# Two table streams in one kernel: a shorter lag, fetches over 8 tokens, routing of all but one head inside the stream

## The chip, the cores and the metric

The kernel runs on one core of one Trainium2 chip. The metric is the time of one execution on the device, in microseconds. The core's engines are named as in the profile: PE is TensorE, DVE is VectorE, ACT is ScalarE, POOL is GpSimd, SP is SyncE. PE, DVE, ACT and POOL each execute their own list of instructions in order and wait on semaphores for one another. Data come from HBM through 16 DMA engines; a transfer is issued from the queue of one of the engines, here from SP (weights) and from POOL (table rows).

## The reference

Two transformer blocks for 256 tokens of 2048 values, all in float32. The first has two kinds of attention and, behind them, a mixture of single-row experts; the second has two more mixers. The change lies in the mixture of experts alone. For each token and each of 8 heads it searches 16 experts among 16384, takes the dot of the token with their rows in one table (`expert_u`), and adds up their rows of a second table (`expert_v`) with weights from these dots:

```python
def peer_ffn(h, w_q, sub_keys, expert_u, expert_v):
    q = (hf @ w_q).reshape(t, PEER_HEADS, 2, PEER_HALF).astype(jnp.float32)
    s1 = jnp.einsum('thd,nd->thn', q[:, :, 0], sk[0])
    s2 = jnp.einsum('thd,nd->thn', q[:, :, 1], sk[1])
    v1, i1 = lax.top_k(s1, PEER_TOPK)
    v2, i2 = lax.top_k(s2, PEER_TOPK)
    cand = (v1[..., :, None] + v2[..., None, :]).reshape(t, PEER_HEADS, PEER_TOPK * PEER_TOPK)
    cs, ci = lax.top_k(cand, PEER_TOPK)
    row = jnp.take_along_axis(i1, ci // PEER_TOPK, axis=-1)
    col = jnp.take_along_axis(i2, ci % PEER_TOPK, axis=-1)
    experts = row * PEER_NKEYS + col
    gates = jax.nn.softmax(cs, axis=-1)
    ...
        a = jax.nn.gelu(jnp.einsum('chkd,cd->chk', expert_u[ec], hc).astype(jnp.float32))
        w = (gc * a).astype(hc.dtype)
        return jnp.einsum('chk,chkd->cd', w, expert_v[ec])
```

With 256 tokens, 8 heads and 16 experts these are 32768 rows of 8 KB from each table, 537 MB in all.

## The kernel before, in words

**Projections.** Each projection is a `dense` (L170): the weights come in parts of 512 KB, which SP fetches (L106) into one of four `raw` buffers up to three parts ahead. ACT writes the high half of a part (L109), DVE subtracts it to get the low half (L110, "the subtraction"), both into one of four `hl` buffers, and PE multiplies the two halves with the two halves of the activations in three matmuls (L166 to L168) for each of the two token groups of 128, t = 0 and t = 1. A weight with blocks of 512 columns has two steps of 128 rows in a part, so a block of 2048 rows has eight parts. When a block is complete, its two groups are handed to an evacuation, a generator that the loop advances at every part.

**The mixture of experts, `peer` (L634).** Its query projection `w_qp` has four blocks of 512 columns, two heads each. The evacuation `ev_qp` (L730) copies the block out of PSUM, transposes it on PE, and multiplies with the two sets of keys into scores. For t = 0 the routing (`route`, L682) follows right there, for two heads at once: the top 16 of four rows of 128 scores, of two rows of 256 sums, then the ids, by comparisons and products on DVE. The scores of t = 1 are parked in the fourth quarter of the tile `gslot`. The ids stand in `eidx`, one column for each expert of a token group: a fetch of the first table takes one column, so it brings one expert row for each of 128 tokens ("u"). For the second table 32 ids of each token are transposed into `eidv` (`spread`, L675: a transpose on PE, four copies), so that one fetch brings all 32 experts of four tokens ("v").

**The stream.** `fill` (L773) issues the fetches from POOL (L786) in the order of the list `seq`: u alone at first, and from u36 on one v after each u, 36 behind (`VLAG`). It stops when no buffer is free or the ids of the next u have not been computed. A fetch takes a whole buffer of 1 MB: three quarters of `gslot` and one part of `hj` (`gbc`) while the projection runs, the four `hl` buffers (`hg`) in addition when it has ended, and the quarter with the parked scores when these have been used. During the projection a `hook` after every second part uses one u. `use_u` (L809) is one DVE row, the dot of 128 tokens with their expert rows (L812). After 32 dots of a group, `weights` (L797) makes their weights: gelu on ACT, the product with the gates, `spread`, and one DVE product with a mask into `lw`, the left operands of eight v. `use_v` (L818) takes two v at a time and lets PE add them into four PSUM tiles, eight matmuls for each (L828). A buffer is free again when its dot or its eight matmuls are done. The routing of t = 1 is advanced between the uses, from use 40 on, one block of two heads at a time. In the last 16 uses the `hl` buffers go back to the weights of the next block.

**What sets the order.** PE's and POOL's instructions in the stream stand in the order in which the program is written; those of DVE and ACT are ordered by a scheduler's priorities.

## Time and profile of the kernel before

| | us |
|---|---|
| median of 3 runs (lowest to highest) | 2880.39 (2880.06 to 2881.32) |
| the profiled execution, its own time | 2880.4 |
| its span in the trace | 2878.6 |

| engine | busy us | share of the span |
|---|---|---|
| PE | 2307.9 | 80% |
| DVE | 1679.5 | 58% |
| ACT | 791.2 | 27% |
| POOL | 668.8 | 23% |

The profile is of one execution. All its times count from the start of the span, which is 1.8 us shorter than the execution's time. The shares are means over stages with different limits, so they say little: the table stage, from about 715 to 2060 us, has to be read in stretches. The views used here are the timeline of an engine (start of a row, its duration, the instruction, and in brackets the idle time before it with what ended it), a table of stretches, the waits, and the traffic of the DMA queues. Rows on DVE overlap a little, so distances between starts are better prices than durations.

### The profile page before, as it was taken

Reading aid. Unit: us, or ns where it says so; the run is one execution under the profiler, and the core shown is the slowest. Engines: PE = TensorE matmul, PEld = TensorE weight load, DVE = VectorE, ACT = ScalarE, POOL = GpSimd, SP = SyncE. Lnnn points to the kernel's source line nnn. Section 1 sums busy time; section 2 is a strip of 40 time slices with the busy share of each in tenths; the row PEclk is TensorE's granted clock in tenths of the full one; section 3 lists DMA queues with packets and bytes.
Section 4 is the critical chain, followed back from the end, with each engine's and each line's share of the span. In section 5 each row is a group of like instructions: output and inputs, shape, how many; then the busy total and the mean of one; then the engine's idle time right before and its main releaser. Section 6 shows DMA issues by size and latency. Waiting matters only on the chain.

```text
span 2878.6 us, 26351 instructions
## 1 busy us (share of the span) xinstructions
PE 2307.9 (80%) x9488; PEld 1445.4 (50%) x9488; DVE 1679.5 (58%) x2503; ACT 791.2 (27%) x1245; POOL 668.8 (23%) x570
## 2 busy tenths in 40 slices
PE   9999999999515565556666666657899999999999
PEld 7878788888401111111111111111388888888887
DVE  5665755657999644444445444441365566667754
ACT  6544544444200000000000000000244444447743
POOL 0000000000354554445445353534100000001000
PEclk9999999999857878887787878788999999999999
DMA  7545466555989999999999999999755555553355
GB/s 249 171 146 183 151 225 199 185 187 194 353 325 357 407 422 421 422 421 421 422 421 422 422 421 422 422 421 421 290 193 188 170 172 188 187 174 131 121 183 168
DMA packets 151955, 820.24 MB, mean 285 GB/s; under 512 B 17232, under 2 KB 17264, under 8 KB 85776
## 3 DMA queue, kind: packets, MB, share of 16 engines
q0 software_dynamic: 75360, 543.75, 46.1%
q1 hardware_dynamic: 76464, 274.81, 28.5%
q8 instruction: 74, 1.21, 0.2%
q14 instruction: 57, 0.47, 0.0%
HBM read 816.39 MB, written 2.10 MB: 284 GB/s over the span
## 4 chain that ended last, share of the span: by engine, by line
PE 50%; DMA 22%; issue 14%; DVE 7%; POOL 7%; ACT 0%; SPq 0%; POOLq 0%; DVEq 0%; ACTq 0%
PE acc L167 15%; PE acc L166 15%; PE acc L168 15%; DMA hg<-expert_v,eidv 8%; DMA gslot<-expert_v,eidv 7%; DMA hj<-expert_v,eidv 3%; POOL gslot L786 3%; POOL hg L786 3%; DVE hj L812 2%; DMA gslot<-expert_u,eidx 2%; PE tr L216 1%; PE acc L828 1%; POOL hj L786 1%; DVE hl L110 1%; PE sd L1146 1%
## 5 line engine op out<-in xcount | busy, mean ns | idle before, releaser
L110 DVE TENSOR_TENSOR hl<-raw,hl 128x1024 fp32r<-128x1024 f32 (+1 forms) x516 | 623.3, 1211 | 525.7 <-ACT hl L109 525.2
L109 ACT ACTIVATE hl<-raw 128x1024 fp32r<-128x1024 f32 (+1 forms) x516 | 540.9, 1049 | 765.9 <-PE acc L168 630.7
L166 PE MATMUL acc<-hl,h 128*128 128x512 f32 (+1 forms) x1472 | 580.8, 395 | 3.4 <-ACT hl L109 3.4
L167 PE MATMUL acc<-hl,h 128*128 128x512 f32 (+1 forms) x1472 | 574.4, 390 | 9.7 <-DVE hl L110 9.7
L168 PE MATMUL acc<-hl,h 128*128 128x512 f32 (+1 forms) x1472 | 573.7, 390 | 0.0
L828 PE MATMUL acc<-hg,lw 128*32 128x512 f32 x880 | 410.2, 811 | 199.5 <-DMA hg<-expert_v,eidv 195.7
L828 PE MATMUL acc<-gslot,lw 128*32 128x512 f32 x848 | 413.0, 806 | 176.2 <-DMA gslot<-expert_v,eidv 176.0
L812 DVE CUSTOM_DVE_ANT_0 hj<-gslot,hj 128x2048 f16<-128x2048 f32 x121 | 277.2, 2291 | 239.5 <-DMA gslot<-expert_u,eidx 239.2
L812 DVE CUSTOM_DVE_ANT_0 hj<-hg,hj 128x2048 f16<-128x2048 f32 x116 | 265.6, 2290 | 205.7 <-DMA hg<-expert_u,eidx 205.3
L167 PEld LDWEIGHTS acc<-hl,h 128*128 128x128 f32 x1472 | 277.1, 188 | 70.0 <-DVE hl L110 13.6
L166 PEld LDWEIGHTS acc<-hl,h 128*128 128x128 f32 x1472 | 276.8, 188 | 61.8 <-ACT hl L109 5.0
L168 PEld LDWEIGHTS acc<-hl,h 128*128 128x128 f32 x1472 | 276.7, 188 | 57.3 <-issue 1.3
L828 PEld LDWEIGHTS acc<-hg,lw 128*32 128x32 f32 x880 | 79.9, 139 | 442.5 <-DMA hg<-expert_v,eidv 273.2
L828 PEld LDWEIGHTS acc<-gslot,lw 128*32 128x32 f32 x848 | 80.3, 138 | 398.5 <-DMA gslot<-expert_v,eidv 251.4
L828 PE MATMUL acc<-hj,lw 128*32 128x512 f32 x320 | 208.1, 803 | 89.5 <-DMA hj<-expert_v,eidv 89.4
L799 ACT ACTIVATE dots<-dots 128x32 f32<-128x32 f32 x8 | 1.8, 229 | 985.7 <-DVE dots L812 985.7
L204 POOL TENSOR_TENSOR rs_y<-rs_v,mhalf 128x2 f32<-128x2 f32 (+2 forms) x25 | 30.3, 1213 | 809.8 <-DVE rs_v L203 809.2
L786 POOL DMA_INDIRECT hg<-expert_v,eidv x110 | 141.9, 1290 | 169.7 <-PE acc L828 126.2
L786 POOL DMA_INDIRECT gslot<-expert_v,eidv x106 | 129.5, 1222 | 205.1 <-PE acc L828 165.3
L786 POOL DMA_INDIRECT gslot<-expert_u,eidx x121 | 131.3, 1085 | 184.6 <-issue 71.9
L786 POOL DMA_INDIRECT hg<-expert_u,eidx x116 | 138.8, 1196 | 128.6 <-DMA hg<-expert_v,eidv 29.1
L828 PEld LDWEIGHTS acc<-hj,lw 128*32 128x32 f32 x320 | 39.7, 139 | 194.1 <-DMA hj<-expert_v,eidv 118.9
(304 smaller groups left out, 2377.1 us busy)
## 6 DMA issues: line engine op xcount, KB each, us to landing
raw<-ev_in SPq DMA_DIRECT2D x128, 512.0 KB, 4.5
raw<-od_in SPq DMA_DIRECT2D x72, 512.0 KB, 3.8
raw<-w_gate SPq DMA_DIRECT2D x64, 512.0 KB, 4.3
raw<-w_dqkv SPq DMA_DIRECT2D x48, 512.0 KB, 3.5
raw<-w_out SPq DMA_DIRECT2D x32, 512.0 KB, 3.8
raw<-w_qp SPq DMA_DIRECT2D x32, 512.0 KB, 5.0
raw<-ev_out SPq DMA_DIRECT2D x32, 512.0 KB, 4.3
raw<-od_out SPq DMA_DIRECT2D x32, 512.0 KB, 4.5
```

The lines of the kernel that those rows point to most:

```text
L109: nc.scalar.activation(hi, raw, AF.Copy)
L110: nc.vector.tensor_tensor(lo, raw, hi.bitcast(F32), op=ALU.subtract)
L166: nc.tensor.matmul(o, xh, wh, start=start, stop=False)
L167: nc.tensor.matmul(o, xh, wl, start=False, stop=False)
L168: nc.tensor.matmul(o, xl, wh, start=False, stop=stop)
L204: nc.gpsimd.tensor_tensor(y, v, self.mhalf[:, :n], op=ALU.pow)
L216: self.nc.tensor.transpose(ps[:, j * P:(j + 1) * P], row[:, j * P:(j + 1) * P], self.ident)
L786: nc.gpsimd.indirect_dma_start(out=g[0], out_offset=None, in_=d[table], in_offset=bass.IndirectOffsetOnAxis(ap=ix, axis=0))
L799: nc.scalar.activation(dots[:, t, sl], dots[:, t, sl], AF.Gelu_apprx_tanh)
L812: nc.vector.tensor_tensor_reduce(junk, g[0], hrow[:, t], 1.0, 0.0, op0=ALU.mult, op1=ALU.add, accum_out=dots[:, t, k:k + 1])
L828: nc.tensor.matmul(st["acc"][n][32 * q:32 * q + 32], lws[t, b][:, q, i], g[0][:, n * 512:(n + 1) * 512], start=(x % P < 4), stop=(x % P >= ...
L1146: nc.tensor.matmul(o, pT[:, i * (t + 1) + k], vo[:, k, g * 64:(g + 1) * 64], start=(k == 0), stop=(k == t))
```

## The change

**First block of the query projection.** The first 512 columns become a weight of their own, `w_qa`, of two blocks of 256 columns, one head each. Its parts hold four steps of 128 rows, so they are still 512 KB, and there are 32 parts for the whole projection as before. The first head of t = 0 is routed straight after its scores, without steps of other work in between, and its 16 ids are released as soon as they exist.

**Routing within the stream.** Of the other nine routings, one of a single head may start in the projection, from use 4 on. All others run between the uses of the stream, from use 18 on, one after the other, those of t = 0 first. Their scores are parked in the fourth quarter of `gslot` and a new tile `sc`; the quarter becomes a buffer when the first five have been taken.

**The product of the gain row.** `hrow`, two DVE products of 2048 columns, is made in the third hook; its gain row's space becomes a buffer then.

**Second table.** A fetch covers 8 tokens with 16 experts instead of 4 tokens with 32, the lag is 20 instead of 36, and weights are made for 16 experts at a time. `spread` is now a product with a mask on DVE and a matmul of 16 columns with the new constant `tdiv`; `lw` has half its size, sixteen times, in three buffers.

```diff
-VLAG = 36
+VLAG = 20
...
-        step = 2 if n <= 512 else 1
+        step = 4 if n <= 256 else 2
...
-        for t in range(2):
-            nc.vector.scalar_tensor_tensor(hrow[:, t], xres[:, t], r2[:, t:t + 1], gbc, op0=ALU.mult, op1=ALU.mult)
+        def rows():
+            for t in range(2):
+                nc.vector.scalar_tensor_tensor(hrow[:, t], xres[:, t], r2[:, t:t + 1], gbc, op0=ALU.mult, op1=ALU.mult)
+            free.append((gbc, False))
...
+        order = [(h, n, t) for t in range(2) for h, n in ((0, 1), (1, 1), (2, 2), (4, 2), (6, 2))][1:]
...
-        free = deque([(gslot[:, i], False) for i in range(3)] + [(gbc, False)])
+        free = deque([(gslot[:, i], False) for i in range(3)])
...
-        def spread(dst, src, b, copy):
-            tp = self.tr()
-            nc.tensor.transpose(tp[:, :P], src, self.ident)
-            tv = tp[32 * b:32 * b + 32, :P].rearrange("p (i m) -> p m i", m=4)
-            for m in range(4):
-                copy(dst[32 * m:32 * m + 32], tv[:, m])
...
+        def masked(src, bias):
+            L = self.at([P, 8, 16])
+            nc.vector.scalar_tensor_tensor(L, src.unsqueeze(1).to_broadcast([P, 8, 16]), bias,
+                                           tmod.unsqueeze(2).to_broadcast([P, 8, 16]), op0=ALU.add, op1=ALU.mult)
+            return L
+
+        def spread(L):
+            ps = self.tr()[:, :16]
+            nc.tensor.matmul(ps, L.rearrange("p m s -> p (m s)"), tdiv, start=True, stop=True)
+            return ps
...
+            if hurry:
+                ready[t] = 16 * h0 + n
...
-            spread(eidv[:, t, sl], ef[:, t], b, nc.vector.tensor_copy)
...
+            Ls = [masked(ef[:, t, sh], 0.25) for sh in halves]
+            yield 1
+            for sh, L in zip(halves, Ls):
+                nc.vector.tensor_copy(eidv[:, t, sh], spread(L))
...
+            if first:
+                todo = route(h0, nh, t, ps, True)
+                while ready[t] == 0:
+                    next(todo)
+                yield 1
+                yield from todo
+            else:
+                nc.scalar.activation(score[h0, t], ps, AF.Copy)
+                have.add((h0, t))
...
-            t, b, r = v // P, v // 32 % 4, v % 32
+            t, b, r = v // P, v // 16 % 8, v % 16
...
-            wT = self.small(32, "wT", bufs=2)
-            spread(wT, dots[:, t], b, lambda o, i: nc.scalar.activation(o, i, AF.Copy))
-            lw = pp.tile([P, 4, 8, 32], F32, tag="lw", name="lw", bufs=2)
-            nc.vector.tensor_tensor(lw, vmask.unsqueeze(1).to_broadcast([P, 4, 8, 32]),
-                                    wT.rearrange("p (g i) -> p g i", g=4).unsqueeze(3).to_broadcast([P, 4, 8, 32]), op=ALU.mult)
+            wT = spread(L)
+            yield 1
+            lw = pp.tile([P, 4, 4, 32], F32, tag="lw", name="lw", bufs=3)
+            nc.vector.tensor_tensor(lw, vmask.unsqueeze(1).to_broadcast([P, 4, 4, 32]),
+                                    wT.rearrange("p (g i) -> p g i", g=4).unsqueeze(3).to_broadcast([P, 4, 4, 32]), op=ALU.mult)
...
+        def route_next(use):
+            if late and st["use"] >= use and late[0][::2] in have and not any(x[3] == "late" for x in self.tasks):
+                h, nh, t = late.popleft()
+                self.spawn(route(h, nh, t, score[h, t]), "late")
...
         def hook():
             n[0] += 1
+            if n[0] == 3:
+                rows()
             if n[0] % 2 == 0:
                 step()
+            if len(late) == len(order):
+                route_next(4)
 
         self.hook = hook
+        self.dense(d["w_qa"], self.h2, ev_qa, rate=0.0)
         self.dense(d["w_qp"], self.h2, ev_qp, rate=0.0)
...
-                if st["use"] >= VLAG + 4 and ready[0] == P and not any(x[3] == "late" for x in self.tasks):
...
+                route_next(VLAG - 2)
+                if sc_a is not None and len(late) < len(order) - 5:
+                    free.append((gslot[:, 3], False))
+                    sc_a = None
```

Three places show how instructions move. The first is DVE's list just ahead of the first routing: L659 (new L663) is `hrow`, L224 and L226 write the last rows of the normalised input, L110 is the subtraction of a weight part, and the first MAX begins the routing. Before:

```order
L659 SCALAR_TENSOR_TENSOR hj<-xres,r_5112,hj 128x2048 x2
L226 TENSOR_TENSOR h_4464<-at,h_4464 128x4x128
L224 TENSOR_TENSOR at<-tr,gains 128x512
L110 TENSOR_TENSOR hl<-raw,hl 128x1024
L226 TENSOR_TENSOR h_4464<-at,h_4464 128x4x128
L110 TENSOR_TENSOR hl<-raw,hl 128x1024 x7
L666 MAX rt_v<-sd 128x8
L110 TENSOR_TENSOR hl<-raw,hl 128x1024
```

And in the changed kernel:

```order
L110 TENSOR_TENSOR hl<-raw,hl 128x1024
L663 SCALAR_TENSOR_TENSOR hj<-xres,r_5112,hj 128x2048
L224 TENSOR_TENSOR at<-tr,gains 128x512 x2
L110 TENSOR_TENSOR hl<-raw,hl 128x1024
L226 TENSOR_TENSOR h_4464<-at,h_4464 128x4x128 x2
L663 SCALAR_TENSOR_TENSOR hj<-xres,r_5112,hj 128x2048
L110 TENSOR_TENSOR hl<-raw,hl 128x1024 x2
L680 MAX rt_v<-sd 128x8
L110 TENSOR_TENSOR hl<-raw,hl 128x1024
```

Seven subtractions stood between the second L226 and the first MAX, and both products ahead of the input rows; now one product and two subtractions stand there, and one product ahead.

The second place is the end of that first routing on DVE, from the comparison of candidate numbers (L709, new L728) to the cast into `eidx`, at which the first fetch can be issued. Before:

```order
L709 TENSOR_TENSOR hj<-rt_f,io 128x1024
L110 TENSOR_TENSOR hl<-raw,hl 128x1024
L714 TENSOR_TENSOR hj<-hj,rt_tab 128x1024
L726 RECIPROCAL s_5583<-s_5583 128x2
L716 TENSOR_REDUCE ef<-hj 128x32
L110 TENSOR_TENSOR hl<-raw,hl 128x1024
L717 CAST eidx<-ef 128x32
```

And in the changed kernel:

```order
L728 TENSOR_TENSOR hj<-rt_f,io 128x512
L751 RECIPROCAL s_5407<-s_5407 128x1
L733 TENSOR_TENSOR hj<-hj,rt_tab 128x512
L752 TENSOR_TENSOR gate<-gate,s_5407 128x16
L110 TENSOR_TENSOR hl<-raw,hl 128x1024
L735 TENSOR_REDUCE ef<-hj 128x16
L110 TENSOR_TENSOR hl<-raw,hl 128x1024
L736 CAST eidx<-ef 128x16
```

The operations are the same on half the columns, since one head is routed and not two, with two subtractions among them as before.

The third place is POOL's list of fetches where the second table begins; `hg`, `gslot` and `hj` are the buffers. Before:

```order
L786 DMA hj<-expert_u,eidx 128x2048
L786 DMA hg<-expert_u,eidx 128x2048 x4
L786 DMA gslot<-expert_u,eidx 128x2048 x3
L786 DMA hj<-expert_u,eidx 128x2048
L786 DMA hg<-expert_u,eidx 128x2048
L786 DMA hg<-expert_v,eidv 128x2048
L786 DMA hg<-expert_u,eidx 128x2048
L786 DMA hg<-expert_v,eidv 128x2048
L786 DMA gslot<-expert_u,eidx 128x2048
```

And in the changed kernel:

```order
L827 DMA gslot<-expert_u,eidx 128x2048
L827 DMA hg<-expert_u,eidx 128x2048
L827 DMA gslot<-expert_u,eidx 128x2048
L827 DMA hg<-expert_u,eidx 128x2048 x2
L827 DMA hg<-expert_v,eidv 128x2048
L827 DMA gslot<-expert_u,eidx 128x2048
L827 DMA hj<-expert_v,eidv 128x2048
L827 DMA gslot<-expert_u,eidx 128x2048
L827 DMA gslot<-expert_v,eidv 128x2048
```

The first v came after 37 u and now comes after 21; from there on the two tables alternate in both.

## Rows read from the trace of the kernel before

**Rows 1.** The page, section 2: DMA share, GB/s, 40 slices

```profile
DMA  7545466555989999999999999999755555553355
GB/s 249 171 146 183 151 225 199 185 187 194 353 325 357 407 422 421 422 421 421 422 421 422 422 421 422 422 421 421 290 193 188 170 172 188 187 174 131 121 183 168
```

**Rows 2.** Stretches: length; PE, PEld, DVE, ACT, POOL busy; PEclk; DMA; GB/s

```profile
700.00:720.00 20.00, 20.00 (x99) 16.72 (x97) 18.18 (x46) 9.08 (x12) 3.89 (x4) 1.00 0.55 178
760.00:960.00 200.00, 72.95 (x204) 22.52 (x203) 194.27 (x480) 9.36 (x19) 105.28 (x69) 0.67 0.92 354
860.00:880.00 20.00, 11.62 (x30) 2.33 (x30) 20.00 (x50) 0.23 (x1) 17.16 (x9) 0.73 0.91 338
1100.00:1500.00 400.00, 239.61 (x645) 50.26 (x643) 188.41 (x168) 2.94 (x15) 188.26 (x160) 0.80 1.01 422
2059.00:2878.00 819.00, 812.15 (x3878) 668.28 (x3878) 510.58 (x847) 400.25 (x635) 28.93 (x27) 1.00 0.51 170
```

**Rows 3.** POOL's timeline, first and last fetch: start, us, what [idle before, releaser]

```profile
715.20 1.31 POOL L786 DMA_INDIRECT gslot<-expert_u,eidx  x1 [50.28 <-issue]
...
2053.38 0.94 POOL L786 DMA_INDIRECT hj<-expert_v,eidv  x1 [5.64 <-PE acc L828]
```

**Rows 4.** DVE's timeline, the dots of u0, u39 and u48

```profile
724.51 2.29 DVE L812 CUSTOM_DVE_ANT_0 hj<-gslot,hj 128x2048 f16<-128x2048 f32 x1 [5.55 <-DMA gslot<-expert_u,eidx]
...
874.72 2.28 DVE L812 CUSTOM_DVE_ANT_0 hj<-gslot,hj 128x2048 f16<-128x2048 f32 x1
...
936.18 2.27 DVE L812 CUSTOM_DVE_ANT_0 hj<-hg,hj 128x2048 f16<-128x2048 f32 x1
```

**Rows 5.** PE's timeline, the last pair of v

```profile
2059.01 0.62 PE L828 MATMUL acc<-hj,lw 128*32 128x512 f32 x1 [1.35 <-DMA hj<-expert_v,eidv]
```

**Rows 6.** DMA queues, 715 to 960: packets, MB, share of 16 engines

```profile
q1 hardware_dynamic: 1872, 6.82, 7.9%
```

**Rows 7.** DVE's timeline up to the first expert ids

```profile
670.26 4.62 DVE L659 SCALAR_TENSOR_TENSOR hj<-xres,r,hj 128x2048 f32<-128x2048 f32 x2 [2.31 <-DMA hj<-g_norm]
...
677.74 3.49 DVE L110 TENSOR_TENSOR hl<-raw,hl 128x1024 fp32r<-128x1024 f32 x3
...
692.36 0.30 DVE L666 MAX8 rt_v<-sd 128x8 f32<-128x128 f32 x1 [1.78 <-PE sd L740]
...
714.16 0.17 DVE L717 CAST eidx<-ef 128x32 uint32<-128x32 f32 x1
```

**Rows 8.** PE's timeline between block 0 and its scores

```profile
688.06 0.60 PE L216 MATMUL tr<-ident,ev 128*128 128x128 f32 x4
...
691.27 1.05 PE L740 MATMUL sd<-skT,at 128*128 128x128 f32 x8
```

**Rows 9.** ACT's timeline, the copy of the transposed queries

```profile
689.22 0.58 ACT L736 ACTIVATE at<-tr 128x512 f32<-128x512 f32 x1
```

**Rows 10.** PE's timeline, two matmuls of 320 columns in a row

```profile
61.25 0.31 PE L166 MATMUL acc<-hl,h 128*128 128x320 f32 x1
61.40 0.31 PE L167 MATMUL acc<-hl,h 128*128 128x320 f32 x1
```

**Rows 11.** DVE's timeline, a dot and the row after it

```profile
844.26 2.27 DVE L812 CUSTOM_DVE_ANT_0 hj<-hg,hj 128x2048 f16<-128x2048 f32 x1
846.46 0.08 DVE L812 DVE_READ_ACCUMULATOR2_ANT dots<- 128x1 f32 x1
```

**Rows 12.** DVE, 655 to 960, groups by form: busy us, mean ns, idle before

```profile
L670 DVE FIND_INDEX8 rt_i<-rt_v,at 128x8 uint32<-128x128 f32 x32 | 9.2, 287 | 0.0
```

**Rows 13.** Waits, 960 to 2000: us in total, times, longest

```profile
DVE lw L805 <- ACT wT L803: 43.4, 7, 7.1
...
DVE eidv L680 <- PE tr L677: 12.4, 2, 6.7
```

**Rows 14.** POOL's timeline, issues beside a busy DVE

```profile
863.71 2.17 POOL L786 DMA_INDIRECT gslot<-expert_u,eidx  x1 [0.30 <-issue]
...
942.13 2.87 POOL L786 DMA_INDIRECT hg<-expert_v,eidv  x1 [2.44 <-DVE dots L812]
```

More of the change, by code (lines that the diff above doesn't have):

```diff
@@ new lines, in route, with ev_q @@
+            ready[t] = 16 * h0 + n
+        def ev_q(h0, nh, t, ps):
+            first = h0 + t == 0
+            row = self.ev()[:, :256 * nh]
+            nc.scalar.activation(row, ps, AF.Copy, scale=r2[:, t:t + 1])
+            if not first:
+                yield 1 + t
+            tp = self.transpose4(row, 2 * nh)
+            qT = self.at([P, 4, P])[:, :2 * nh]
+            nc.scalar.activation(qT, tp, AF.Copy)
+            if not first:
+                yield 1
+            ps = self.sd()[:, :256 * nh]
+            for j in range(2 * nh):
+                nc.tensor.matmul(ps[:, j * P:(j + 1) * P], qT[:, j], sk[:, j % 2], start=True, stop=True)
+            if first:
[7 more added lines that the diff above has]
+                have.add((h0, t))
@@ L1237, in consts @@
     out["kdec"] = np.ascontiguousarray((np.exp(lg[None, :] * (127.0 - i[:, None])) / 16.0).astype(f))
[L1238 to L1242 removed]
+    vm = np.zeros((8, 16, 4, 32), f)
+    for m in range(8):
+        for i_ in range(4):
+            vm[m, :, i_, 8 * i_ + m] = 1.0
+    out["vmask"] = vm.reshape(P, 4, 32)
+    out["tmod"] = np.ascontiguousarray((i[:, None] % 8 == np.arange(8)[None, :]).astype(f))
+    out["tdiv"] = np.ascontiguousarray((i[:, None] // 8 == np.arange(16)[None, :]).astype(f))
     return out
```

109 lines of the change are left out of this document (50 added, 59 removed).

## The prediction

> **What bounds the kernel now.** Start with the slices of the whole span: from slice 15 to slice 28 of 72 us the DMA row shows 9 and the GB/s row 421 to 422, while slices 11 to 14 reach only 325 to 407, and no other gets to 300 [rows 1]. That is the table stage: 256 fetches of the first table ("u", each used by one DVE dot) and 256 of the second ("v", used in pairs by TensorE), 1,048,576 bytes each. At 421.5 GB/s one fetch takes 1.0486 / 0.4215 = **2.488 us** of all 16 DMA engines, 512 of them 1273.8 us. The table by stretches says the same: 422 GB/s from 1100 to 1500 with DVE at 188 of 400 us, but 354 GB/s from 760 to 960 with DVE at 194.27 of 200, and after 2059 PE at 812 of 819 us with DMA half idle [rows 2]. So there are three limits in a row: until the first fetch a chain on PE and DVE; then DVE, for about 200 us; then DMA up to the last fetch. What follows the last fetch is PE work that the change does not touch.
>
> The stage can be written as one sum, for the time at which the last pair of v starts on PE:
>
> first issue + 6.8 + 1273.8 + R x 1.62 + lost.
>
> The 6.8 is the latency of the first fetch without its own transfer: issue at 715.20, use at 724.51 [rows 3, 4], 9.3 - 2.49. R counts the 512 KB weight parts that share the engines after the first issue: 6.82 MB on the weight queue between 715 and 960 [rows 6] are 13 parts. A part costs what 700 to 720 shows: 0.55 of 20 us for 178 x 20 = 3.56 MB, 6.8 parts [rows 2], so 11 / 6.8 = 1.62 us. Before: 715.2 + 6.8 + 1273.8 + 21.1 = 2016.9. The last pair starts at 2059.01 [rows 5], so **42.1 us are lost**, DMA time that nothing used. From 760 to 960 alone it is (422 - 354) / 422 x 200 = 32.2 [rows 2]; the other 9.9 lie in the start, in the dense stage up to 760 and behind the last issues [rows 3].
>
> **The change part by part.** *First issue.* Now block 0 of the query projection is 256 columns and one head. Its inputs: DVE begins at 670.26 when the gain row has landed [rows 7]. Ahead of the last rows of h2 there now stands one of the two 2.31 us products instead of both, then one subtraction (3.49 / 3 = 1.16 [rows 7]) and two L224 and two L226 of half its size, some 0.6 each (an estimate from it): 676.2. The last part of block 0 is then 24 matmuls. None of 256 columns is in the trace; those of 320 columns follow each other after 0.15 us [rows 10], which bounds one from above, and by columns it is 0.12 (an estimate): 2.9 us, 679.1. Then copy out (0.6, like the copy below), transpose to its copy (688.06 to 689.22, 1.16), that copy (0.58), scores to MAX8 (691.27 to 692.36, 1.09) [rows 7 to 9]: 3.4, so MAX8 at 682.5 against 692.36. From there to the ids it was 21.8 us (692.36 to 714.16 [rows 7]) with seven subtractions in the DVE order between, 3.11 us per subtraction; they come at the pace of the weight parts. One head has half the routing work, and five subtractions stand between now: 5 x 3.11 = 15.6, ids at 698.1, first issue 1.04 later as before [rows 3, 7]: **699.2, 16.0 us earlier**.
>
> *Parts moved behind it.* Of the 32 subtractions of the projection 20 stood ahead of the ids, now 13. So seven more parts share the engines with the fetches, R = 20: **+11.3 us**. The earlier start is thus worth only 5.
>
> *Lost time.* Until u35 the old stream used u alone: each 2.488 us of fetching brought DVE a dot of 2.20 us [rows 11] plus its share of routing. With VLAG 20 every second fetch from u20 on is a v that asks nothing of DVE. In the old trace u39 starts at 874.72 and u48 at 936.18 [rows 4]: 6.83 us for a u with routing around it. That is over a u and a v (4.98) too, but the earlier 36 u put DVE behind first. I added up the DVE rows in the new order, each at its duration from the rows by form (a search in 128 values 0.287 [rows 12], less the overlap with the next row); the same count for the old order gives 209.8 us from u0 to u48, where the trace has 936.18 - 724.51 = 211.7 [rows 4]. New, from u0: u27 at 115.5, u37 at 158, u52 at 216, u63 at 243. DMA needs up to the same u, with its share of the parts: 117, 165, 240, 295. So DMA is last from start to end, narrowly until u27. The loss that remains comes from lumps: the order has routing between consecutive u in four stretches, of about 4, 2, 4 and 4 dots at 6.83 against 4.98, so DVE falls behind by 7.4, 3.7, 7.4 and 7.4. Eight buffers hold 8 x 2.488 = 19.9 us of fetches; less 9.3 of latency [rows 3, 4] and 1.9 for an issue (below) a lag of 8.7 drains nothing. By that nothing is lost at all. But two kinds of DVE rows stand behind PE: the casts of `eidv`, and `lw`, which now reads the result of the spread matmul straight from PSUM. DVE executes in order, so the dots behind them wait too, and with them the buffers that they free. The old waits of this kind are 43.4 us in 7 and 12.4 in 2 [rows 13], 6.2 each, about a pair of v at the low clock. One such wait in a stretch makes 7.4 + 6.2 - 8.7 = 4.9. I take it in two of the stretches: 10 us; with none it is 0, with one in each and a second in two of them 22. So of 32.2, 10 are left: **-22.2**, bounds -32 and -10.
>
> *What costs nothing.* The mask product of each 16 ids or weights (128 elements, 0.2 us, x32), 16 instead of 8 `lw` at half the size, and 16-column matmuls instead of transposes: DVE has over 200 of 400 us idle after 960 [rows 2], and PE waits for v there. If that cover were gone they would cost some 6 us. The four copies per spread on DVE or ACT go. At the end 20 v follow the last u instead of 36, and the last `lw` has 4 v (10 us) of cover against a wait of 6.2: nothing.
>
> *Sum.* 699.2 + 6.8 + 1273.8 + 32.4 + 9.9 + 10 = 2032.1 against 2059.0: -26.9. The profiled execution took 2880.4 with a span of 2878.6, and the median of the runs is 2880.39, so no correction: **2853.5 us**.
>
> **The rivals.** *A, the forecast*: 2843.5 to 2865.5 with the bounds of the lumps. *B, the lumps keep all they had*: DVE stays the bound up to u60, say because the 12 dots in the projection hold its subtractions and thus the dense stage; 32.2 lost again gives 2875.7. For it speaks that the count is narrow until u27, against it the 24 us by which DVE is ahead at u52. *C, no lump drains the buffers*: 2843.5. *D, slower: POOL falls behind.* Every fetch is issued by POOL, and while DVE is busy an issue is longer: from 860 to 880, with DVE at 20.00 of 20, nine issues took 17.16 us [rows 2], 1.9 each and 2.2 with the 0.3 between [rows 14]. A fetch takes 2.488, so this still keeps up. But the new order puts some 88 fetches (u18 to u63 with their v) beside the routing, where the old one ran u alone, often waiting for buffers. If the mean there is that of the long ones, 2.87 [rows 14], each is 3.17 - 2.49 = 0.68 late, 60 us in all: 2913.5. It decides once issues average over 2.19 us; it eats the whole gain of 27 once they average 2.5, since 88 x 0.31 = 27. For it: with the gaps those nine fill 19.9 of the 20 us, so POOL had nothing to spare there; against it: nine fetches in 20 us are more than DMA can carry, 8. [...] *E, the first issue is not earlier*: parts or h2's rows hold block 0, as L110 held the old one, and it comes at 713: +14, 2867.5.
>
> **How the numbers follow.** A 0.60, C 0.16, E 0.08, B 0.10, D 0.06. The predicted time is A's. The range covers A, C and E, with 2 us below C since the 9.9 of other losses may shrink as well: 2841 to 2870; B and D, 0.16, are outside. A measurement of this kernel can tell about 0.2%, 5.8 us, from no change. Faster by more are A, C and E, 0.84; within are B's, 0.10; slower is D, 0.06.
>
> **What would show it.** The first issue on POOL near 699 and the first MAX8 on DVE near 683 (E: near 713). In the table by stretches over 400 GB/s from about 770 on, with short drops where the routing stands, DVE near full only until u27 (B: 340 GB/s up to 960 again). POOL's mean issue below 2.2 us between 780 and 960 (D: above, with POOL at 20 of 20 and DVE waiting for DMA). Waits of DVE's `lw` and `eidv` rows for the spread matmul, some of 6 us. The last pair of v near 2032, and everything from there to the end 27 us earlier and as long as before. I am wrong if the stage after 1000 falls below 420 GB/s: then the lag of 20 leaves weights or ids late, a cause that no term here holds.

## The result, and the profile after

The changed kernel takes **2849.86 us** (median of 4 runs, 2846.25 to 2851.50) against 2880.22 us of the kernel before beside it (2879.65 to 2881.32): a ratio of 0.9892, 95% interval 0.9875 to 0.9910, 30.4 us. In a second comparison (below, five rounds) it took 2852.02 us, ratio 0.9890 (0.9873 to 0.9906). The profiled execution took 2846.25 us, the fastest of its four, with a span of 2844.5.

The head of the page and its 40 slices, of the changed kernel; a slice is now 71 us and the table stage begins in the tenth:

```profile
span 2844.5 us, 26683 instructions
...
DMA  7545466556999999999999999999755455553355
GB/s 249 176 148 175 151 225 199 187 186 239 380 394 403 399 410 422 422 421 422 422 421 422 422 422 422 422 421 422 272 179 194 161 177 188 189 180 119 120 186 168
```

Slices 11 to 14 stand at 380 to 403 GB/s, where [rows 1] has 325 to 407. The same in stretches, columns as in [rows 2]:

```profile
760.00:960.00 200.00, 123.40 (x365) 36.34 (x365) 167.10 (x446) 15.00 (x23) 100.95 (x77) 0.80 0.98 404
780.00:960.00 180.00, 107.71 (x286) 23.77 (x288) 150.40 (x419) 7.50 (x13) 86.02 (x69) 0.78 0.98 403
960.00:1100.00 140.00, 83.82 (x232) 18.71 (x228) 99.44 (x185) 4.16 (x7) 75.38 (x58) 0.80 0.99 405
1000.00:1100.00 100.00, 60.83 (x172) 14.01 (x172) 72.89 (x157) 3.46 (x6) 49.40 (x40) 0.80 1.01 413
2026.00:2844.00 818.00, 811.65 (x3878) 667.86 (x3874) 510.67 (x847) 400.45 (x635) 28.92 (x27) 1.00 0.51 170
```

From 760 to 960 the engines now move 404 GB/s, not 354, with DVE busy 167.10 of 200 us, not 194.27. From 960 to 1100 it is 405, where the old kernel had reached 422: a part of the routing has moved there. From 1000 to 1100 it is 413, under the 420 that the prediction named as a sign that it is wrong (what is behind it stands in the section on why the prediction was right). From the last pair of v on, nothing has changed: 818 us with PE busy 811.65.

The start of the stage on POOL and on DVE (product of the gain row, first MAX8, cast of the first ids, first dot), then the last pair of v on PE, and the bytes of the weight queue from 693 to 960:

```profile
693.21 1.07 POOL L827 DMA_INDIRECT gslot<-expert_u,eidx  x1 [27.86 <-DVE eidv L748]
```

```profile
667.62 2.35 DVE L663 SCALAR_TENSOR_TENSOR hj<-xres,r,hj 128x2048 f32<-128x2048 f32 x1 [0.33 <-DMA hj<-g_norm]
...
678.52 0.29 DVE L680 MAX8 rt_v<-sd 128x8 f32<-128x128 f32 x1
...
692.17 0.17 DVE L736 CAST eidx<-ef 128x16 uint32<-128x16 f32 x1
...
702.43 2.29 DVE L854 CUSTOM_DVE_ANT_0 hj<-gslot,hj 128x2048 f16<-128x2048 f32 x1 [4.05 <-DMA gslot<-expert_u,eidx]
```

```profile
2025.54 0.62 PE L870 MATMUL acc<-gslot,lw 128*32 128x512 f32 x1 [1.35 <-DMA gslot<-expert_v,eidv]
```

```profile
q1 hardware_dynamic: 2940, 10.67, 11.1%
```

The first fetch is issued at 693.21 where [rows 3] has 715.20, the last pair of v starts at 2025.54 where [rows 5] has 2059.01. With a fetch at 2.488 us as before and 10.67 MB = 20.4 weight parts at 1.62, the sum of the prediction is 693.2 + 6.8 + 1273.8 + 33.0 = 2006.8, so 18.7 us of DMA time are lost, where the kernel before lost 42.1.

### The profile page after: what moved, and what is told of

Its sections match the earlier page's. It is cut to its first block, busy times and chain, and to the rows that moved or that the text cites. A ratio compares the mean times of both kernels' runs of the same rounds, so it can differ in the third digit from the quotient of the medians.

```text
span 2844.5 us, 26683 instructions
## 1 busy us (share of the span) xinstructions
PE 2341.2 (82%) x9632; PEld 1461.7 (51%) x9632; DVE 1692.7 (60%) x2563; ACT 797.6 (28%) x1238; POOL 669.4 (24%) x572
## 3 DMA queue, kind: packets, MB, share of 16 engines
q8 instruction: 75, 1.23, 0.2%
## 4 chain that ended last, share of the span: by engine, by line
PE 52%; DMA 22%; issue 12%; POOL 7%; DVE 5%; ACT 0%; SPq 0%; POOLq 0%; ACTq 0%; DVEq 0%
PE acc L167 15%; PE acc L166 15%; PE acc L168 15%; DMA gslot<-expert_v,eidv 9%; DMA hg<-expert_v,eidv 7%; POOL gslot L827 3%; DMA hj<-expert_v,eidv 3%; POOL hg L827 3%; PE acc L870 2%; DMA gslot<-expert_u,eidx 2%; DVE hj L854 2%; PE tr L216 1%; PE sd L1196 1%; POOL hj L827 1%; DVE hl L110 1%
## 5 line engine op out<-in xcount | busy, mean ns | idle before, releaser
L110 DVE TENSOR_TENSOR hl<-raw,hl 128x1024 fp32r<-128x1024 f32 (+1 forms) x516 | 623.2, 1211 | 489.5 <-ACT hl L109 488.7
L870 PE MATMUL acc<-hg,lw 128*32 128x512 f32 x1112 | 523.9, 834 | 258.4 <-DMA hg<-expert_v,eidv 258.4
L166 PE MATMUL acc<-hl,h 128*128 128x512 f32 (+2 forms) x1504 | 587.1, 391 | 3.4 <-ACT hl L109 3.4
L167 PE MATMUL acc<-hl,h 128*128 128x512 f32 (+2 forms) x1504 | 581.5, 387 | 8.4 <-DVE hl L110 8.4
L168 PE MATMUL acc<-hl,h 128*128 128x512 f32 (+2 forms) x1504 | 580.3, 386 | 0.0
L854 DVE CUSTOM_DVE_ANT_0 hj<-gslot,hj 128x2048 f16<-128x2048 f32 x161 | 368.6, 2289 | 286.6 <-DMA gslot<-expert_u,eidx 285.8
L870 PE MATMUL acc<-gslot,lw 128*32 128x512 f32 x616 | 332.8, 819 | 127.6 <-DMA gslot<-expert_v,eidv 127.6
L870 PEld LDWEIGHTS acc<-hg,lw 128*32 128x32 f32 x1112 | 102.7, 142 | 572.8 <-DMA hg<-expert_v,eidv 348.6
L167 PEld LDWEIGHTS acc<-hl,h 128*128 128x128 f32 x1504 | 284.1, 189 | 67.6 <-DVE hl L110 12.5
L166 PEld LDWEIGHTS acc<-hl,h 128*128 128x128 f32 x1504 | 284.0, 189 | 60.9 <-ACT hl L109 4.3
L168 PEld LDWEIGHTS acc<-hl,h 128*128 128x128 f32 x1504 | 283.9, 189 | 56.6 <-issue 1.3
L854 DVE CUSTOM_DVE_ANT_0 hj<-hg,hj 128x2048 f16<-128x2048 f32 x76 | 173.9, 2289 | 123.5 <-DMA hg<-expert_u,eidx 123.3
L827 POOL DMA_INDIRECT hg<-expert_v,eidv x139 | 182.9, 1316 | 231.3 <-PE acc L870 165.7
L827 POOL DMA_INDIRECT gslot<-expert_u,eidx x161 | 174.2, 1082 | 232.3 <-DVE dots L854 53.9
L204 POOL TENSOR_TENSOR rs_y<-rs_v,mhalf 128x2 f32<-128x2 f32 (+2 forms) x25 | 30.4, 1216 | 806.3 <-DVE rs_v L203 803.5
L827 POOL DMA_INDIRECT hg<-expert_u,eidx x76 | 84.4, 1110 | 44.7 <-issue 18.9
```

The costliest lines, as they stand in the source:

```text
L110: nc.vector.tensor_tensor(lo, raw, hi.bitcast(F32), op=ALU.subtract)
L166: nc.tensor.matmul(o, xh, wh, start=start, stop=False)
L167: nc.tensor.matmul(o, xh, wl, start=False, stop=False)
L168: nc.tensor.matmul(o, xl, wh, start=False, stop=stop)
L204: nc.gpsimd.tensor_tensor(y, v, self.mhalf[:, :n], op=ALU.pow)
L827: nc.gpsimd.indirect_dma_start(out=g[0], out_offset=None, in_=d[table], in_offset=bass.IndirectOffsetOnAxis(ap=ix, axis=0))
```

## The experiments

All are edits of the changed kernel or of one of the others, and each was compared with the kernel before on its own chip, so the ratios are what to compare; medians of one kernel differ by some 2 us between the comparisons. "Stream" is the rate from 760 to 1100; its shortfall against 422 GB/s times 340 us is the time lost there.

| kernel | median us | ratio to before (95%) | first fetch | 693 to 760, GB/s | stream, GB/s | lost in the stream, us | last pair |
|---|---|---|---|---|---|---|---|
| before | 2880.2 | 1 | 715.2 | 262 | 382 | 32.2 | 2059.0 |
| changed | 2849.9 | 0.9892 (0.9875 to 0.9910) | 693.2 | 361 | 404 | 14.5 | 2025.5 |
| changed, again | 2852.0 | 0.9890 (0.9873 to 0.9906) | 696.6 | 345 | 401 | 16.9 | 2031.7 |
| lag 36 | 2860.1 | 0.9918 (0.9900 to 0.9935) | 693.7 | 360 | 389 | 26.6 | 2037.9 |
| one block of two heads | 2854.3 | 0.9896 (0.9879 to 0.9914) | 714.5 | 318 | 402 | 16.1 | 2034.6 |
| routing in the projection | 2871.1 | 0.9961 (0.9946 to 0.9976) | 691.9 | 332 | 381 | 33.0 | 2047.7 |
| 8-token fetches alone | 2873.0 | 0.9960 (0.9946 to 0.9975) | 710.6 | 311 | 381 | 33.0 | 2051.9 |
| ACT takes the spread results | 2854.2 | 0.9902 (0.9885 to 0.9918) | 694.7 | 339 | 401 | 16.9 | 2031.7 |
| both products first | 2848.0 | 0.9881 (0.9864 to 0.9898) | 693.8 | 361 | 404 | 14.5 | 2025.7 |
| routing at half the pace | 2843.7 | 0.9868 (0.9851 to 0.9884) | 693.0 | 361 | 413 | 7.3 | 2020.8 |
| routing at twice the pace | 2851.6 | 0.9895 (0.9879 to 0.9912) | 696.4 | 359 | 401 | 16.9 | 2031.2 |
| half pace, one block of two heads | 2854.0 | 0.9902 (0.9885 to 0.9918) | 709.7 | 346 | 401 | 16.9 | 2035.2 |
| half pace, both products first | 2844.4 | 0.9868 (0.9851 to 0.9884) | 696.0 | 353 | 411 | 8.9 | 2023.7 |
| half pace, DVE in written order | 2844.2 | 0.9872 (0.9856 to 0.9889) | 692.0 | 352 | 419 | 2.4 | 2019.4 |

**The lag put back.**

```diff
-VLAG = 20
+VLAG = 36
...
-                route_next(VLAG - 2)
+                route_next(18)
```

> The changed kernel with the lag put back to 36; everything else, the place of the routing (from use 18) too, as changed. Theory (the lag's use is that every second fetch is a v, which asks DVE for nothing, while DVE routes): the stretch u20 to u35 is u alone beside routing again, DVE falls behind (row count: u37 at 141 us from u0 on DVE against 127 on DMA, changed kernel 158 against 167), so some 15 us of DMA time are lost there again: about 2865 us, first fetch near 693 as in the changed kernel, GB/s well under 400 between 760 and 860. Rival (the lag does nothing, the place of the routing does): 2850 us, as the changed kernel.

Its stretches from 760 on:

```profile
760.00:800.00 40.00, 16.91 (x84) 13.57 (x83) 36.91 (x77) 8.27 (x12) 26.62 (x16) 0.78 1.01 415
800.00:860.00 60.00, 10.15 (x42) 4.07 (x42) 59.08 (x145) 3.24 (x5) 23.70 (x16) 0.55 0.79 295
860.00:960.00 100.00, 61.70 (x156) 12.98 (x156) 89.24 (x248) 4.96 (x8) 52.61 (x40) 0.74 0.98 393
```

From 800 to 860, where the stream is u alone beside routing, the rate falls to 295 GB/s with DVE at 59.08 of 60; the changed kernel has 389 there. The stream loses 12.1 us more than in the changed kernel, the time is 8 us longer by the ratios (0.0027 of 2880), where the theory has 15 and the rival nothing. The intervals of the ratios overlap a little, but all four executions of this kernel (2857.8 to 2861.1) lie above all eight of the changed one (2846.1 to 2853.7). The lag does what the theory says, at about half of the size in the time.

**One block of two heads again.**

```diff
-        self.dense(d["w_qa"], self.h2, ev_qa, rate=0.0)
         self.dense(d["w_qp"], self.h2, ev_qp, rate=0.0)
...
-            return ev_q(2 + 2 * b, 2, t, ps)
+            return ev_q(2 * b, 2, t, ps)
```

> The changed kernel with the first 512 query columns as one block of two heads again, both routed at once in a hurry; lag, 8-token fetches and the routing in the stream as changed. Theory (an earlier first fetch is mostly paid back by the weight parts that then share the engines): first fetch near 708, 15 us later than in the changed kernel; seven parts less beside the fetches, 11 us; lumps the same: 4 us longer, 2854 us. Rival (the first fetch is worth what it is earlier): 2865 us.

POOL's first fetch, and PE's last pair, of this run:

```profile
714.48 2.07 POOL L827 DMA_INDIRECT gslot<-expert_u,eidx  x1 [45.09 <-DVE eidv L748]
```

```profile
2034.61 0.62 PE L870 MATMUL acc<-gslot,lw 128*32 128x512 f32 x1 [1.35 <-DMA gslot<-expert_v,eidv]
```

The first fetch comes 18 to 21 us later than in the two profiles of the changed kernel, the last pair 2.9 to 9.1 later, and by the ratios the time is 1 to 2 us longer, with intervals of 10 us. (The other two kernels with this block fetch first at 709.7 and 710.6, so some 5 us of the 18 to 21 can be the scatter of one profile.) So of 18 to 21 us in the first fetch, most is not seen at the end, as the theory has it: the weight parts that now lie ahead of the fetches no longer lie beside them.

**The routing of the first 128 tokens back in the projection.**

```diff
+            elif t == 0:
+                yield from route(h0, nh, t, ps)
             else:
                 nc.scalar.activation(score[h0, t], ps, AF.Copy)
...
-            if len(late) == len(order):
-                route_next(4)
```

> The changed kernel with the routing of all heads of the first 128 tokens inside the projection as before, straight after each block; only the other group's routing in the stream. Theory (routing beside u alone and weight parts puts DVE behind before the v begin): row count u27 at 131 us from u0 on DVE against 120 on DMA, 15 us of DMA time lost again: 2865 us. Rival (where the routing stands does not matter with a lag of 20): 2850 us.

```profile
693.00:760.00 67.00, 58.83 (x276) 47.78 (x275) 59.47 (x136) 24.10 (x30) 15.88 (x13) 0.97 0.87 332
760.00:1100.00 340.00, 185.47 (x559) 54.54 (x557) 248.38 (x566) 16.84 (x26) 166.74 (x126) 0.76 0.95 381
```

With the early first fetch and the lag of 20 in place, 332 and 381 GB/s: the stream loses 33 us again, as before the change (32.2). The time is 20 us longer than the changed kernel's by the ratios. This is the largest of the parts that were undone.

**The second table, nearly alone.** The kernel before with fetches over 8 tokens (the gain-row product stays in the third hook, and the first block is routed without steps of other work in between): the three edits above together, the other group's routing from use 40 on as before.

```diff
-VLAG = 20
+VLAG = 36
...
-        self.dense(d["w_qa"], self.h2, ev_qa, rate=0.0)
         self.dense(d["w_qp"], self.h2, ev_qp, rate=0.0)
...
+            elif t == 0:
+                yield from route(h0, nh, t, ps)
...
-                route_next(VLAG - 2)
+                route_next(40)
```

> The kernel before with the second-table part of the change alone: fetches over 8 tokens and 16 experts, weights for 16 experts, the mask product and the 16-column matmul; lag 36, one block of two heads first, routing in the projection. (The gain-row product stays in the third hook and the first two heads are routed in a hurry.) Theory (8-token fetches by themselves cost and bring nothing, they only allow the lag of 20): 2880 us less the 3 to 6 us by which the first fetch is earlier without the two products ahead of it and with no steps between, 2875 us. Rival 1 (shorter runs of the mask and copies are themselves a gain on DVE of 15 us or more): below 2866 us. Rival 2 (the 16 spread matmuls behind v on PE, for which DVE waits in order, cost): above 2882 us.

0.9960, 11.5 us faster than before. The first fetch is 4.6 us earlier (710.6) and the stream loses what it lost before (33.0 against 32.2), so some 7 of the 11.5 us stand in the last pair (2051.9 against 2059.0); they are won ahead of 760, where 311 GB/s for 262 are 7.8 us of DMA time. The theory's 5 us are below the interval (7 to 16 us), the rivals are off on both sides; the rest of the 11.5 is in no row, the two profiled executions being 6.6 us apart.

**Which cause for what is still lost.** The changed kernel again as an anchor on the same chip, and three edits.

> The changed kernel itself, run beside the next three on one chip as their anchor: 2850 us, ratio 0.989 to the kernel before.

The first edit lets ACT and not DVE take the results of the spread matmuls:

```diff
-                nc.vector.tensor_copy(eidv[:, t, sh], spread(L))
+                nc.scalar.activation(eidv[:, t, sh], spread(L), AF.Copy)
...
-            wT = spread(L)
-            yield 1
+            wT = self.small(16, "wT", bufs=2)
+            nc.scalar.activation(wT, spread(L), AF.Copy)
+            yield 2
```

> The changed kernel with no DVE row behind the spread matmul: ACT casts the ids into eidv and copies the spread weights to SBUF, and the product into lw comes two uses later. Theory 1 (the DMA time that is still lost after 760 comes from DVE rows that wait for PE in order, two of them 6 us each in the stretches with routing): 5 to 9 us shorter, 2843 us, and no wait of eidv or lw for PE in the list of waits. Theory 2 (it comes from routing rows in a row between two dots, after which the freed buffers are issued by POOL one after the other at 2 to 2.9 us): the waits go, the time stays, 2850 us.

The waits of the changed kernel between 760 and 1100 (total, times, longest), then of this one, and the stream of this one and of the anchor:

```profile
DVE lw L847 <- PE tr L697: 15.6, 4, 4.6
...
DVE eidv L748 <- PE tr L697: 8.0, 2, 7.0
```

```profile
ACT eidv L748 <- PE tr L697: 126.4, 7, 45.8
...
DVE at L682 <- PE tr L697: 22.1, 5, 5.9
```

```profile
760.00:1100.00 340.00, 207.11 (x604) 58.27 (x604) 266.59 (x616) 24.41 (x50) 179.26 (x133) 0.79 0.99 401
```

```profile
760.00:1100.00 340.00, 206.96 (x600) 57.35 (x600) 267.08 (x629) 20.48 (x31) 179.60 (x132) 0.78 0.98 401
```

ACT waits now, but DVE still does: 22.1 us in five waits for the same matmuls, where the changed kernel has 23.6 in six. The next search that writes a tile `at` (L682) has to wait, since the matmul reads the masked ids or weights out of such a tile. The stream has 401 GB/s in both. So the edit moved the waits and did not take them away, and this run does not decide between the theories.

The second edit lets the routings in the stream, but for the first, advance at every second use:

```diff
+            pace = 1 if hurry or (h0, t) in ((1, 0), (2, 0)) else 2
...
-                yield 1
+                yield pace
```

> The changed kernel with the routings in the stream, but for the first, advanced at every second use of u instead of at every one, so that half as many routing rows stand between two dots (per u some 2.2 + 2.3 us of DVE against 4.98 us for a u and a v). Theory 2: DMA time lost between 840 and 1000 goes, 5 to 10 us shorter, 2841 us, GB/s at 420 in the stretches 860 to 960 and 960 to 1100; the loss of 820 to 840, where the first routing stands, stays. Theory 1: 2850 us.

```profile
760.00:1100.00 340.00, 211.69 (x600) 55.44 (x599) 233.97 (x495) 19.74 (x27) 174.71 (x134) 0.79 1.00 413
```

413 GB/s, 9.6 us less lost in the stream than the anchor, and 8.3 us less time (2843.7 against 2852.0 on one chip): theory 2 within its range. The drop at 820 to 840 went too (413 GB/s there, 336 in the anchor), which the expectation had not thought. DVE's waits for PE are as long as ever:

```profile
DVE lw L848 <- PE tr L697: 19.1, 4, 5.8
DVE eidv L749 <- PE tr L697: 4.7, 4, 1.8
```

These 23.8 us (21.7 in the anchor) with half the loss show that the waits alone do not make it: less routing between two dots is enough to halve it. They do not show that the waits cost nothing. The 420 GB/s expected from 860 to 960 did not come: it is 401, with drops at 870 and 950, each behind a stretch with such a wait (see the next section).

The third puts both gain-row products ahead of the projection:

```diff
-            if n[0] == 3:
-                rows()
...
+        rows()
```

> The changed kernel with both gain-row products ahead of the projection again instead of in its third hook. Theory (h2's last rows stand behind them on DVE, and block 0 behind these): first MAX8 and first fetch 2.3 to 4.7 us later, 696 to 698, and the time longer by as much less one part, 2852 us. Rival (block 0 is held by something else, weight parts or PE): first fetch at 693 and 2850 us.

DVE's products, first MAX8 and first ids of this run:

```profile
667.40 4.61 DVE L663 SCALAR_TENSOR_TENSOR hj<-xres,r,hj 128x2048 f32<-128x2048 f32 x2 [0.54 <-DMA hj<-g_norm]
...
680.30 0.29 DVE L682 MAX8 rt_v<-sd 128x8 f32<-128x128 f32 x1
...
692.75 0.17 DVE L738 CAST eidx<-ef 128x16 uint32<-128x16 f32 x1
```

The ids follow the start of the products by 25.4 us, in the changed kernel by 24.6 (667.62 to 692.17) and in the anchor by 25.8. So nothing of 2.3 to 4.7 us is seen in the first fetch, nor in the time: there the rival holds. The first MAX8 does come later, 12.9 us after the start of the products for 10.9 (12.1 in the anchor), but the ids follow it after 12.45 us and not 13.65, since one subtraction less stands in between.

**Denser, evener, and once more the first block.** Twice the pace instead of half of it:

```diff
-                yield 1
+                if j % 2 or hurry:
+                    yield 1
```

> The changed kernel with the routings in the stream made denser, two of their steps at each use of u where it has one. Theory 2 (DMA time is lost where many routing rows stand between two dots): by the row count DVE is behind the fetches from u27 (119 us from u0 against 115) to u52 (244 against 240), some 12 us lost more, 2863 us, with GB/s under 380 between 800 and 900. Rival (the even pace helps for another reason, such as less routing beside the last heads): 2851 us.

Its stretches, then the anchor's:

```profile
800.00:860.00 60.00, 28.53 (x96) 8.10 (x96) 58.87 (x189) 3.24 (x5) 25.89 (x21) 0.72 0.91 363
860.00:960.00 100.00, 62.06 (x166) 14.13 (x168) 93.34 (x285) 4.20 (x9) 46.62 (x39) 0.76 0.97 395
960.00:1100.00 140.00, 87.05 (x234) 18.81 (x232) 72.77 (x74) 1.41 (x3) 69.90 (x58) 0.78 1.01 421
```

```profile
800.00:860.00 60.00, 34.73 (x96) 7.86 (x98) 51.62 (x143) 3.24 (x5) 28.23 (x22) 0.81 0.95 393
860.00:960.00 100.00, 58.57 (x164) 13.07 (x160) 76.76 (x205) 3.44 (x6) 48.27 (x37) 0.82 0.99 403
960.00:1100.00 140.00, 86.04 (x224) 18.96 (x226) 101.84 (x204) 4.97 (x8) 79.87 (x57) 0.72 0.98 400
```

The loss is where the theory put it, 14.8 us between 800 and 960 against 8.6 in the anchor. But from 960 on 0.3 is lost, where the anchor loses 7.3, and the time is the anchor's. The 12 us more were wrong: in this run a denser routing gathers the loss and does not add to it.

The written order on DVE, on top of half the pace and of ACT's copies:

```diff
-        with self.tc.manual_schedule(engines={mybir.EngineType.PE, mybir.EngineType.Pool}):
+        with self.tc.manual_schedule(engines={mybir.EngineType.PE, mybir.EngineType.Pool, mybir.EngineType.DVE}):
```

> The same kernel (routing steps at every second use) with DVE's rows in the stream kept in the order in which they are written, not the scheduler's, and with ACT taking the results of the spread matmuls out of PSUM. Theory 2: the scheduler gathers routing rows into clumps of up to 4.8 us between two dots; in the written order none is over 3.3 us, so the losses left between 860 and 980 (about 6 us) go: 2838 us and 420 GB/s in every stretch from 760 to 1100. Rival (what is left is POOL's issue, of about a dot's length beside a dot): 2844 us.

```profile
760.00:1100.00 340.00, 211.13 (x608) 56.18 (x606) 241.50 (x454) 22.82 (x42) 175.37 (x139) 0.80 1.01 419
1100.00:1500.00 400.00, 250.28 (x678) 55.75 (x678) 240.84 (x355) 15.61 (x36) 187.98 (x160) 0.78 1.01 418
```

419 GB/s in the stream and 420 to 423 in every 20 us from 780 to 1100: nothing is left there to lose, as theory 2 says. But no wait of DVE for PE is left in this stretch either, so the run takes away both causes at once and does not separate them. The time does not follow: 2844.2 us, four runs from 2841.3 to 2847.0. Of the 5 us won in the stream about 3 go between 1100 and 1500 (418 GB/s for 421), and the profiled execution lost some 3 more before 780 than the kernel without this edit (304 GB/s from 720 to 740 for 346, 384 from 760 to 780 for 412).

Half the pace together with the edit of the first block, and together with both products first (the diffs are those above):

> The kernel with routing steps at every second use (the one that took 2844 us, ratio 0.987) with the first 512 columns as one block of two heads again. Theory (of an earlier first fetch the weight parts behind it take back most): first fetch near 713, 20 us later, seven parts less beside the fetches (11 us), so 5 to 9 us longer: 2851 us, ratio 0.989 to 0.990. Rival (earlier fetches are worth what they are earlier): 2864 us. Rival 2 (nothing): 2844 us.

> The same kernel (routing steps at every second use) with both gain-row products ahead of the projection. Theory (after the run that tried this alone: the first fetch does not depend on them within 1 us): 2844 us; rival (2.3 us later scores, one 1 MB buffer from the start on): 2842 to 2847 us, both hard to tell apart.

The products again show nothing (0.9868 as without). The block shows 9.6 us between these two kernels, with first fetches 13.7 apart. That is just above the theory's 5 to 9 us, but not by its mechanism alone: the kernel with the block of two heads also loses 8 us more in the stream (401 against 411 GB/s). 4.8 us are lost in it from 1040 to 1080 alone (371 GB/s), behind a wait of DVE for PE of 6.6 us, and from 1100 to 1500 another 5 more than in the other kernel (416 for 421). Why it loses there was not tested.

## Why the prediction was right

The forecast was 2853.5 us, the measured median 2849.9, and case A of the prediction is what happened. Term by term, against the profiled execution:

| term | forecast, us | trace, us |
|---|---|---|
| first issue | -16.0 | -22.0 |
| weight parts beside the fetches | +11.3 | +12.0 |
| lost in the stream | 32.2 to 10 | 32.2 to 14.5 |
| lost elsewhere | 9.9, unchanged | 4.2 |
| all | -26.9 | -33.5 |

The second profile of the changed kernel, of an execution of 2853.7 us, has -18.6, +12.2, 32.2 to 16.9 and 9.9 to 4.3 for these terms and the last pair at 2031.7, next to the forecast's 2032.1. So the terms of one profile are good to a few us.

*The first issue* was mis-sized by 6. The ids followed the first MAX8 after 13.65 us, not 15.6. The prediction took a pace of 3.11 us per weight part from the old stretch; but DVE is busy there for 21.46 of 21.60 us, and in the new one for 13.50 of 13.70, so the ids come when DVE has done its rows, half the routing and five subtractions. The run with both products first bears this out: one subtraction less, 1.2 us less. The MAX8 followed the gain row after 10.9, not 12.2 (12.1 in the second profile). The last 2.6 are no effect of the change: the gain row itself landed at 667.6 in this execution and at 670.26 in the old one [rows 7]. In eight profiles of kernels with the same code up to there the first fetch came between 691.9 and 696.6, so a single profile tells it to some 5 us. The step in which one product instead of two stood ahead of h2's rows was wrong as a cause of the earlier first fetch: with both ahead the ids come as early, within the scatter.

*The payback* was right in the trace, 7.4 parts more for the 7 of the order, and the run with two heads in one block bears it out: 18 to 21 us in the first fetch were worth 1 to 2 us by the ratios (with half the pace 14 us were worth 10, with the stream at fault for part of it).

*The lost time* came out right for a sum of two wrong halves, which is luck. The other losses fell by 5.7, which the forecast had left alone: from 740 to 760, in the projection, the old kernel moves 252 GB/s, 8 us lost, and the changed one 361, 3 us. And in the stream 14.5 us are left, not 10, in four drops of the rate, as there were four lumps. The sum that the prediction made for a lump, lag plus wait for PE less what the buffers cover, can be followed in the trace. Count from a dot that waited for its rows to land: each u after it takes 4.98 us of fetching with its v, and what DVE takes beyond that is how far it is behind. The last columns are the rate after it and the DMA time that this lost:

| kernel | from a dot to a dot | u | behind, us | last wait for PE in it, us | GB/s, from to | lost, us |
|---|---|---|---|---|---|---|
| changed | 841.30 to 881.12 | 6 | 10.0 | 4.6 | 356, 880 to 900 | 3.1 |
| changed | 904.34 to 917.30 | 1 | 8.0 | 7.0 | 423, 910 to 930 | 0 |
| changed | 904.34 to 966.33 | 10 | 12.2 | 3.6 | 383, 960 to 1000 | 3.7 |
| changed | 1008.11 to 1045.39 | 5 | 12.4 | 4.6 | 401, 1040 to 1080 | 2.0 |
| half pace | 838.04 to 867.01 | 4 | 9.1 | 4.6 | 367, 870 to 890 | 2.6 |
| half pace | 920.19 to 950.15 | 4 | 10.1 | 4.5 | 378, 950 to 980 | 3.1 |
| half pace | 1002.42 to 1025.93 | 3 | 8.6 | 5.8 | 415, 1020 to 1040 | 0.3 |

The wait and the last two dots of the first of these:

```profile
849.37 0.69 DVE L847 TENSOR_TENSOR lw<-vmask,tr 128x512 f32<-128x512 f32 x1 [4.59 <-PE tr L697]
...
875.29 2.27 DVE L854 CUSTOM_DVE_ANT_0 hj<-hg,hj 128x2048 f16<-128x2048 f32 x1
...
881.12 2.27 DVE L854 CUSTOM_DVE_ANT_0 hj<-gslot,hj 128x2048 f16<-128x2048 f32 x1
```

8.0 us behind cost nothing here, 8.6 next to nothing, 9 to 12 cost 2 to 4. So the cover of 8.7 was near what these stretches show. The waits were mis-sized, 3.6 to 4.6 us and not 6.2, and three of the four lumps have one, not two. The last row but three explains the 413 GB/s from 1000 to 1100: it is routing and a wait for PE, and not the lag of 20, with which the kernel in written order has 421 to 422 there.

The fourth drop, from 820 to 830 (228 GB/s, 4.6 us), is where the step failed: the prediction held that lags without a wait drain nothing. Four dots stand 6.5 to 7.0 us apart there, up to 817.88, DVE is 7.9 us behind by the same count (three of the u were fetched alone), and no wait for PE is in it. Its last two dots, POOL's issues, and PE's last matmuls with the buffer `hj`:

```profile
811.38 2.27 DVE L854 CUSTOM_DVE_ANT_0 hj<-hg,hj 128x2048 f16<-128x2048 f32 x1
...
817.88 2.27 DVE L854 CUSTOM_DVE_ANT_0 hj<-hg,hj 128x2048 f16<-128x2048 f32 x1
```

```profile
813.93 0.94 POOL L827 DMA_INDIRECT hg<-expert_u,eidx  x1 [3.15 <-DVE at L682]
820.43 2.87 POOL L827 DMA_INDIRECT hg<-expert_v,eidv  x1 [5.56 <-DVE dots L854]
...
824.84 0.95 POOL L827 DMA_INDIRECT hj<-expert_v,eidv  x1 [0.30 <-issue]
```

```profile
814.26 1.02 PE L870 MATMUL acc<-hj,lw 128*32 128x512 f32 x2
```

Between two dots DVE does 4.2 us of routing, 6.5 from start to start. POOL waits from 814.87 to 820.43 for a buffer that a dot frees, and then issues beside the next dot, 2.87 us for 0.94. All that time from 815.28 on the buffer `hj` is empty; since POOL's issues stand in written order, its next fetch comes at 824.84, behind the one that waits. So the cover is not one number. Whether this order or rows that have landed and wait for PE made it smaller here was not tested.

What share of the 14.5 us the waits have is not shown either, since no run took them away alone: ACT's copies moved them, half the pace left them and halved the loss, and the written order took away both them and the lumps (16.9 lost in the anchor, then 7.3, then 2.4). The prediction's bound for more waits does not come out of its own rule: one in each lump and a second in two of them are 28 us, not 22. Neither was reached.

*Where the gain lies among the edits.* The prediction put the 22 us to the lag above all. The runs put more to the place of the routing: undone alone it costs 20 us, the lag 8, the first block 1 to 2. With the 11.5 of the kernel with 8-token fetches, of which the forecast had none, that is more than the 30 that there are, so the parts are not independent.

*The rivals.* B and E did not occur; E moreover counted 14 us for a later first fetch without the weight parts that are then no longer beside the fetches; the run with two heads shows that most of such a delay comes back. C would have been 2843.5, which is the time with half the pace of routing, but by other terms: 7.3 us are still lost in its stream. The longer issues of D are there (up to 2.87 us beside a dot, in the last section), but beside dots POOL issues one fetch per dot, 2.33 us apart, which is under the 2.49 of a fetch, and in the mean from 780 to 960 an issue takes 1.25 us (86.02 in 69): POOL keeps up.

## What to carry to other kernels

Write the time of a streaming stage as first issue + latency + bytes at the full rate + lost, and take each term from rows: an earlier start is only worth what does not then run beside the stream (here 18 to 21 us in the first fetch were worth 1 to 2 us). Work that shares an engine with the consumers of a stream must be cut so that what stands between two consumers fits into the time of a transfer (4.98 us for a u and its v here; stretches that left DVE 9.1 to 12.4 us behind lost 2.0 to 3.7). That count takes in the waits for PE, the last ones 3.6 to 7.0 us long; what share of the loss they have was not shown. An edit that is to take a wait away has to be checked in the list of waits: here it came back at the next row that needed the same tile. Half the pace of routing is an edit of four lines and gave 2843.7 us, 8.3 less than the changed kernel beside it.

## What the runs showed of the hardware

From 760 to 1100 of the changed kernel, no issue of an indirect fetch that POOL began while DVE ran a dot was done before the dot was. DVE's dots and POOL's issues from 883 on:

```profile
883.43 2.29 DVE L854 CUSTOM_DVE_ANT_0 hj<-gslot,hj 128x2048 f16<-128x2048 f32 x1
...
885.76 2.29 DVE L854 CUSTOM_DVE_ANT_0 hj<-hg,hj 128x2048 f16<-128x2048 f32 x1
...
888.10 2.29 DVE L854 CUSTOM_DVE_ANT_0 hj<-hg,hj 128x2048 f16<-128x2048 f32 x1
```

```profile
883.66 2.87 POOL L827 DMA_INDIRECT gslot<-expert_v,eidv  x1 [4.89 <-DVE dots L854]
886.84 2.03 POOL L827 DMA_INDIRECT hg<-expert_u,eidx  x1 [0.31 <-issue]
889.17 2.03 POOL L827 DMA_INDIRECT hj<-expert_v,eidv  x1 [0.30 <-issue]
891.51 0.94 POOL L827 DMA_INDIRECT gslot<-expert_u,eidx  x1 [0.30 <-issue]
```

The three issues that begin within a dot end at 886.53, 888.87 and 891.20, the dots at 885.72, 888.05 and 890.39: 0.81 to 0.82 us later each time, whatever the issue's duration (2.03 to 2.87). From 760 to 1100 that holds for 35 issues, all between 0.80 and 0.82 us behind a dot's end. The 17 that began up to 0.6 us ahead of a dot ran on into it and took 0.93 to 0.94, and the other 82 take 0.99 us in the mean. The dot is not the only row of which this holds. Four issues began within a row of the routing with two operands in SBUF (L728, L733, 0.68 to 1.23 us); they took 1.14 to 1.78 us and ended 0.80 to 0.82 us behind the row. One of them:

```profile
825.46 1.22 DVE L728 TENSOR_TENSOR hj<-rt_f,io 128x1024 f32<-128x1024 f32 x1
```

```profile
826.10 1.40 POOL L827 DMA_INDIRECT gslot<-expert_u,eidx  x1 [0.30 <-issue]
```

This issue ends at 827.50, 0.82 us behind the row. Within the reductions of one operand (L735) and the product `lw` with one operand in PSUM (L847) it was not so: the eight issues that began within one of them took 0.93 to 0.94. The dot has two operands in SBUF as well, a fetched row and `hrow`. Whether it is this that made the issues longer was not tested. That an issue which began first makes a dot longer is not seen: the 17 dots that began within one took 2.29 us in the mean, the others 2.28.
